# Tiles moved to whole kilobytes of SBUF, and a loop order changed in two places of a diffusion block's small matmuls

## Chip, cores and metric

The kernel runs on one core of one Trainium2 chip. The metric is the time on the device of one execution, in microseconds (us); lower is better. The profile names the engines PE (TensorE; PEld is its loading of weights), DVE (VectorE), ACT (ScalarE), POOL (GpSimd) and SP (the queue that issues most DMAs).

## What is computed

A block of two layers works on 1024 latent tokens and 256 context tokens of width 1024. The first layer is attention (differential attention in 4 heads and neighbourhood attention in 8), the second a bidirectional state-space layer (S5) followed by a GLU; both layers end in an MLP with a hidden width of 4096. Cut to the parts that matter here:

```python
# first layer: y = concat(diff_attention, neighbourhood_attention) @ w_out ; x = x + g1*y
# second layer, for both directions:
bur = einsum('blgh,gph->blgp', u, bbr); bui = einsum('blgh,gph->blgp', u, bbi)   # 64 groups of 16 channels, 64 states
s   = scan(a, bu)                                                               # complex, along the tokens
y  += einsum('blgp,ghp->blgh', sr, c_re) - einsum('blgp,ghp->blgh', si, c_im)
z   = gelu(y + d*h);  x = x + g1 * (z @ w_a) * sigmoid(z @ w_b)
# both layers:
x   = x + g2 * (square(relu(h2 @ w1)) @ w2)
```

## The kernel before

**Large products.** Every large product is made of three float32r products in `mm3` (L309 to L316): the weights and the activations are each split into a high and a low part (`w_hi`, `w_lo`; `Hh`, `Hl`, or `hid_h`, `hid_l` for the hidden layer), and hi x hi, hi x lo and lo x hi are added in PSUM. The weights are the stationary operand, 128 x 128, the activations stream past them, 512 tokens at a time (256 for the block of context tokens). Only `vv` (L541) is the other way round: there the activations are stationary and the weights stream, `wh[:, :, k]`, two runs of 128 columns, each 512 bytes in a partition. Weights come through two pools: `raw` (as loaded, 1024 columns) and `wp` (split, two buffers, L298 to L307).

**Stages.** The input projection (`in_proj`, L454; accumulators `ip_acc` and `v_acc`) runs to 512 us; between its products the generator `prep` (L1642) puts in the preparation of the state-space layer: the adaLN vectors (`ada`, L243, accumulator `ada_acc`) and, 16 times, `ssm_slice` (L1269). Then come attention (to 967 us; its order is written by a planner with costs and ranks, `Plan`, which orders each engine's work), the output projection (`op_acc`), the first MLP (`mlp`, L1120, `m_acc`), from 2036 us the scan of the state-space layer (`ssm`, L1403, planned in the same way), the GLU (`g_acc`, 2257 to 2443 us) and the second MLP. Outside the planner's stages each engine works in the order of the program.

**The lag kernels.** `ssm_slice` builds, for four groups q of 16 channels, a kernel over lags: matmuls of 64 states (rows 0 to 63 or 64 to 127 of the array, by q % 2) and 32 output channels (columns 32q of the array and partitions 32q of one PSUM tile, `sl_kp`). For each q there are three stretches of lags (128, 16 and 112 columns), each with a real and an imaginary part `ri`; operands are plain float32, which makes two instructions of each matmul. The results are copied out (`sl_ks`) and stored for the scan. The same array can hold several such small matmuls at once, each in its own tile of rows and columns.

**The scan's inputs.** In `ssm`, `xmm` (L1472) projects two groups g2 into the states of the scan: the array's columns and the PSUM partitions 64 g2, 128 rows. Direction d = 0 has one matmul of 160 tokens for each g2 and ri; d = 1 has two, of 32 and 128 tokens, read backwards.

**Where tiles lie.** SBUF is shared out by pools that grow from the left end or from the right end; a pool opened on top of others lies next to them, and tiles lie in a pool in the order of their allocation. Start addresses that the program's allocation gives, in bytes of a partition, and what they are beyond a whole kilobyte (1024 bytes):

| tiles | side | start | beyond a kilobyte |
|---|---|---|---|
| Hh, Hl of the first layer | left | 20416, 36800, ... 94144 | 960 |
| w_hi, w_lo | left | 28608, 44992, ... | 960 (each second 128 columns: 448) |
| hid_h, hid_l, both layers | left | 143296, ... 61376, ... | 960 |
| Hh, Hl of the second layer | right | 120288, 136672, 153056, 169440 | 480 |
| attention: p, k, v, q | right | 147872, ... | 416 |

Each row of 512 float32 tokens is 2048 bytes, so that all rows of a tile begin at the same offset. The constants' pool, which the change touches in `setup` (L209), lies at the left end below all others; the pool of `u_norm` (L1353, `rp`) is opened on the right before the second layer's `H1`.

Of the kernel before, what the change touches and what calls it, by code (L numbers as in the profile page):

```python
# [9 lines left out]
F32 = mybir.dt.float32  # L10
# [7 lines left out]
P = 128  # L18
# [182 lines left out]
class Net:  # L201
# [7 lines left out]
    def setup(self, es):  # L209
        nc, a = self.nc, self.a  # L210
        self.cp = es.enter_context(self.pool("const"))
        cp = self.cp
        cv = cp.tile([P, KT, 2], F32, name="cv")
        nc.sync.dma_start(cv, a["cvec"])
        self.vecs = cp.tile([P, 137], F32, name="vecs")
        nc.gpsimd.dma_start(self.vecs, a["vecs"])
        self.ident = cp.tile([P, P], F32, name="ident")
        make_identity(nc, self.ident)

        self.fold = cp.tile([P, 2], F32, name="fold")  # L220
        nc.vector.tensor_reduce(self.fold, self.ident.rearrange("p (q m) -> p m q", q=4)[:, 0:2], axis=AX.X, op=ALU.add)
        self.ones32 = cp.tile([P, 32], F32, name="ones32")
        nc.vector.memset(self.ones32, 1.0)
        self.inv32 = cp.tile([P, 1], F32, name="inv32")
        nc.vector.memset(self.inv32, 1.0 / 32.0)
        self.mhalf = cp.tile([P, 8], F32, name="mhalf")
        nc.vector.memset(self.mhalf, -0.5)
        self.act = cp.tile([P, KT, 32], F32, name="act")
        nc.vector.memset(self.act, 0.0)
        nc.scalar.activation(self.act[:, :, 0:2], cv, AF.Silu)  # L230
        self.hm = cp.tile([P, 16], F32, name="hm")
        nc.gpsimd.dma_start(self.hm, a["k_hm"])
        self.sd = cp.tile([P, 16], F32, name="sd")
        nc.gpsimd.dma_start(self.sd, a["s_d"])
        self.m = [cp.tile([P, 48, 2], F32, name=f"m{i}") for i in range(2)]
        self.G1 = [cp.tile([P, 8, 2], F32, name=f"G1_{i}") for i in range(2)]
        self.G2 = [cp.tile([P, 8, 2], F32, name=f"G2_{i}") for i in range(2)]
# [446 lines left out]
    def attention(self, at, ps):  # L684
# [20 lines left out]
                   pv=[bank[3].rearrange("p (u t) -> p u t", u=4)])  # L705
        turn = dict.fromkeys(mem, 0)
        sq = at.tile([P, P], F32, name="at_sq")

        def T(ring):
            turn[ring] += 1  # L710
# [44 lines left out]
        for h in range(4):  # L755
# [3 lines left out]
            for b, (t0, n) in enumerate(BLK):  # L759
# [4 lines left out]
                for u in range(nq):  # L764
                    st = {}
# [159 lines left out]
                o = [plan.add("S", 0.29, r + 0.5, F(g2, u=u), [o1]) for u in range(nq)]  # L925
                o = plan.add("V", 0.6, r + 1, g3, o)
                o = plan.add("G", 0.9, r + 1, g4, [o])
                o = plan.add("V", 0.47, r + 2, g5, [o])
                o = [plan.add("G", 0.35, r + 2, F(gn, u=u), [o], give=[("s0", first)]) for u in range(nq)]
                o6 = plan.add("PE", 0.11 * nq, r + 5, g6, o, take=["tp"], give=[("on", o1)])  # L930
                o = plan.add("S", 0.13 + 0.11 * nq, r + 4, g7, [o6])
# [4 lines left out]
        for pr in range(4):  # L936
# [3 lines left out]
            for rp in range(10):  # L940
                b, u = (rp // 4, rp % 4) if rp < 8 else (2, rp - 8)
# [9 lines left out]
                st = {}  # L951
# [72 lines left out]
                for hh in range(2):  # L1024
                    q = rank + (2.35 if big else 0.5) * hh
# [9 lines left out]
                for i in range((nk + 511) // 512):  # L1035
                    c, w = 512 * i, min(512, nk - 512 * i)
                    evs = []
                    for hh in range(2):
                        q = rank + 8 + 2 * i + hh
# [229 lines left out]
    def ssm_slice(self, sl, pz, ps):  # L1269

        nc, a = self.nc, self.a
        V, G = nc.vector, nc.gpsimd
        cols = slice(4 * sl, 4 * sl + 4)
        bc = pz.tile([P, 4, 4, 16], F32, name="sl_bc", tag="sl_bc", bufs=2)
        nc.sync.dma_start(bc.rearrange("p q c h -> p q (c h)"), a["s_bc"][sl])

        def big(w):
            return pz.tile([P, 576], F32, name="sl_big", tag="big", bufs=4)[:, :w]

        bb = pz.tile([P, 2, 4, 32], F32, name="sl_bb", tag="sl_bb", bufs=2)  # L1280
        V.memset(bb[:, :, :, 16:32], 0.0)
        tb = pz.tile([P, 4, 16], F32, name="sl_tb", tag="sl_tb", bufs=2)
        cf = [self.cf[:, q, cols][:, :, None].broadcast_to([P, 4, 16]) for q in range(2)]
        self.cmul(V, (bb[:, 0, :, 0:16], bb[:, 1, :, 0:16]), cf, (bc[:, 0], bc[:, 1]), tb)

        bl = [big(512).rearrange("p (a s h) -> p a s h", a=4, s=8) for _ in range(2)]
        t = big(512).rearrange("p (a s h) -> p a s h", a=4, s=8)
        sh = [P, 4, 8, 16]
        pw = [self.pB[:, q, cols][:, :, :, None].broadcast_to(sh) for q in range(2)]
        bv = [bb[:, q, :, 0:16][:, :, None, :].broadcast_to(sh) for q in range(2)]  # L1290
        self.cmul(V, bl, pw, bv, t)
        yield
        st = pz.tile([P, 4, 2, P], F32, name="sl_st", tag="sl_st", bufs=1)
        for h in range(2):
            tp = ps.tile([P, 512], F32, name="sl_tp", tag="mm")
            for q in range(4):
                nc.tensor.transpose(tp[:, P * q:P * q + P], bl[q % 2][:, 2 * h + q // 2].rearrange("p s h -> p (s h)"), self.ident)
            nc.scalar.activation(st[:, 2 * h:2 * h + 2].rearrange("p c r m -> p (c r m)"), tp, AF.Copy)
        nc.sync.dma_start(self.pD[:, 2 * sl:2 * sl + 2, 0:512], st.rearrange("p (a c) r m -> p a (c r m)", a=2))

        nci = pz.tile([P, 4, 16], F32, name="sl_nci", tag="sl_nci", bufs=2)
        V.tensor_scalar(nci, bc[:, 3], -1.0, None, op0=ALU.mult)
        sh = [P, 4, 9, 16]
        w = pz.tile([P, 4, 2, 144], F32, name="sl_w", tag="sl_w", bufs=1)
        wv = w.rearrange("p c r (j h) -> p r c j h", j=9)
        t = [big(576).rearrange("p (a j h) -> p a j h", a=4, j=9) for _ in range(2)]
        pw = [self.pC[:, q, cols][:, :, :, None].broadcast_to(sh) for q in range(2)]
        cr, ci, ni = (x[:, :, None, :].broadcast_to(sh) for x in (bc[:, 2], bc[:, 3], nci))
        G.tensor_tensor(wv[:, 0], pw[0], cr, ALU.mult)
        V.tensor_tensor(t[0], pw[1], ci, ALU.mult)  # L1310
        G.tensor_tensor(wv[:, 0], wv[:, 0], t[0], ALU.subtract)
        G.tensor_tensor(wv[:, 1], pw[0], ni, ALU.mult)
        V.tensor_tensor(t[1], pw[1], cr, ALU.mult)
        G.tensor_tensor(wv[:, 1], wv[:, 1], t[1], ALU.subtract)
        nc.sync.dma_start(self.pD[:, 2 * sl:2 * sl + 2, 512:1088], w.rearrange("p (a c) r m -> p a (c r m)", a=2))
        yield

        kp = ps.tile([P, 512], F32, name="sl_kp", tag="mm")
        for q in range(4):
            o, ln = kp[32 * q:32 * q + 32], slice(64 * (q % 2), 64 * (q % 2) + 64)  # L1320
            c = 2 * (q // 2)
            for lo, hi, d, w0, start, stop in ((0, 128, 1, 16, True, False), (112, 128, 0, 0, False, True), (128, 240, 0, 16, True, True)):
                for ri in range(2):
                    nc.tensor.matmul(o[:, lo:hi], bb[ln, ri, c + d], w[ln, c + d, ri, w0:w0 + hi - lo], start=start and ri == 0,
                                     stop=stop and ri == 1, skip_group_check=True)
        ks = pz.tile([P, 240], F32, name="sl_ks", tag="sl_ks", bufs=2)
        V.tensor_copy(ks, kp[:, :240])
        V.scalar_tensor_tensor(ks[:, 112:128], self.hm, self.sd[:, sl:sl + 1], ks[:, 112:128], op0=ALU.mult, op1=ALU.add)
        for q in range(4):
            nc.sync.dma_start(self.KD[:, 4 * sl + q], ks[32 * q:32 * q + 16])  # L1330
        yield
# [21 lines left out]
    def u_norm(self, rp, sp, ps):  # L1353
# [5 lines left out]
        for q, v in enumerate((self.G1[1], self.m[1][:, 0:8])):  # L1359
            nc.sync.dma_start(gD[q].rearrange("c g h m -> (g h) c m"), v)  # L1360
        self.gU = rp.tile([P, 2, 64, 2], F32, name="gU")
        for s in range(8):
            for q in range(2):
                nc.sync.dma_start(self.gU[16 * s:16 * s + 16, q], gD[q].rearrange("c g h m -> h (c g) m"))
# [38 lines left out]
    def ssm(self, sp, ps):  # L1403
# [24 lines left out]
        for pair in range(32):  # L1428
# [43 lines left out]
            def xmm(st=st, pair=pair, ct=ct, pl=pl):  # L1472
                bl = st["par"][:, 0:512].rearrange("p (d r m) -> p d r m", d=2, r=2)
                st["U"] = U_of[ct]
                X = st["X"] = T("X")
                for ri in range(2):
                    for d in range(2):
                        for g2 in range(2):
                            U = st["U"][:, 2 * pl + g2]

                            for c, u in ((0, U),) if d == 0 else ((160, U[:, 31::-1]), (192, U[:, 159:31:-1])):
                                PE.matmul(X[64 * g2:64 * g2 + 64, ri, c:c + u.shape[1]], bl[:, d, ri, 64 * g2:64 * g2 + 64], u,
                                          start=True, stop=True, skip_group_check=True)

# [242 lines left out]
```

## Time and profile before

| | us |
|---|---|
| median of 3 runs | 3184.99 (3183.87 to 3185.97) |
| profiled execution | 3183.76 |
| its span, first to last instruction | 3181.7 |
| PE busy in the span | 2997.4 (94%), 17736 matmuls |
| DVE, POOL, ACT busy | 1848.8, 1129.1, 969.6 |
| mean granted clock of TensorE | 0.978 of full speed |

A row of a group gives line, engine, operation, what is written and read, shape and count; then the busy time, the mean length of one in ns, and the engine's idle time before them. Matmuls are pipelined: the length of one goes on while the next has begun, so that the time that one costs is read from start to start. A row of the timeline gives the start, the length, the instruction and how many of the line stand together there. A row of a stretch gives its length, then for each engine the busy time and the count, the granted clock, the DMA engines' share and GB/s.

### The profile page before, as it was taken

How to read it: one execution, taken by the hardware profiler on the slowest of the kernel's cores; microseconds unless marked ns; L12 is line 12 of the kernel's file. 1: busy time of each engine (PE TensorE's matmuls, PEld its weight loads, DVE VectorE, ACT ScalarE, POOL GpSimd, SP SyncE). 2: the span in 40 equal slices, each digit the busy share in tenths (PEclk: the TensorE clock that was granted, in tenths of full speed). 3: DMA queues.
4: the chain of work that ended last, by engine and by line, in shares of the span. 5: the costliest groups of instructions: out<-in, count | busy, mean ns of one | idle time of the engine just before them, and what ended most of it. 6: DMA issues, size and time to landing. Idle time of an engine off the chain costs nothing.

```text
span 3181.7 us, 46326 instructions
## 1 busy us (share of the span) xinstructions
PE 2997.4 (94%) x17736; PEld 2470.1 (78%) x17736; DVE 1848.8 (58%) x3225; ACT 969.6 (30%) x1843; POOL 1129.1 (35%) x2314
## 2 busy tenths in 40 slices
PE   7999998888999999999999999777899999999998
PEld 4878888777878777877888888566677888888886
DVE  4886575998663555445555454599524544455444
ACT  3321114766663311221111211455323212111122
POOL 3352123555442377778785000377323000000001
PEclk8999999999999999999999999888999999999999
DMA  6355565233543133333311111666212111111111
GB/s 234 106 195 200 198 203 151 67 89 101 153 113 133 60 124 104 117 104 110 60 62 53 34 33 38 165 186 177 85 60 86 48 45 53 40 54 48 45 53 53
DMA packets 171150, 321.55 MB, mean 101 GB/s; under 512 B 34560, under 2 KB 97056, under 8 KB 170928
## 3 DMA queue, kind: packets, MB, share of 16 engines
q1 hardware_dynamic: 165840, 302.24, 30.9%
q0 software_dynamic: 5088, 16.34, 1.7%
q8 instruction: 140, 2.29, 0.3%
q14 instruction: 82, 0.67, 0.1%
HBM read 253.03 MB, written 65.49 MB: 100 GB/s over the span
## 4 chain that ended last, share of the span: by engine, by line
PE 67%; DVE 10%; issue 2%; ACT 2%; DMA 2%; POOL 1%; SPq 0%; DVEq 0%; POOLq 0%; ACTq 0%
PE m_acc L314 17%; PE m_acc L315 16%; PE m_acc L316 16%; PE at_bank L736 2%; DVE s_ab L1501 2%; PE at_sc L728 2%; PE g_acc L314 2%; PE g_acc L316 2%; PE g_acc L315 2%; PE at_bank L1019 2%; DVE s_ab L1489 1%; PE at_bank L846 1%; PE ada_acc L266 1%; PE op_acc L316 1%; DVE s_s L1514 1%
## 5 line engine op out<-in xcount | busy, mean ns | idle before, releaser
L1087 DVE SCALAR_TENSOR_TENSOR xl<-m_acc,m,xl 128x512 f32<-128x512 f32 x512 | 379.1, 748 | 222.3 <-PE m_acc L316 221.6
L314 PE MATMUL m_acc<-Hh,w_hi 128*128 128x512 f32 (+1 forms) x1280 | 476.1, 372 | 0.9 <-ACT Hh L450 0.9
L314 PE MATMUL m_acc<-hid_h,w_hi 128*128 128x512 f32 (+1 forms) x1280 | 476.8, 372 | 0.0
L315 PE MATMUL m_acc<-Hl,w_hi 128*128 128x512 f32 (+1 forms) x1280 | 474.4, 371 | 0.5 <-DVE Hl L451 0.5
L316 PE MATMUL m_acc<-Hh,w_lo 128*128 128x512 f32 (+1 forms) x1280 | 474.1, 370 | 0.0
L315 PE MATMUL m_acc<-hid_l,w_hi 128*128 128x512 f32 (+1 forms) x1280 | 471.9, 369 | 0.0
L316 PE MATMUL m_acc<-hid_h,w_lo 128*128 128x512 f32 (+1 forms) x1280 | 471.6, 368 | 0.0
L305 ACT ACTIVATE w_hi<-w_raw 128x1024 fp32r<-128x1024 f32 x196 | 202.6, 1053 | 803.7 <-PE m_acc L315 691.5
L306 DVE TENSOR_TENSOR w_lo<-w_raw,w_hi 128x1024 fp32r<-128x1024 f32 x196 | 243.6, 1257 | 219.9 <-ACT w_hi L305 210.3
L1138 DVE TENSOR_TENSOR m_r<-m_r 128x512 f32<-128x512 f32 (+1 forms) x160 | 105.7, 662 | 414.2 <-ACT hid_h L1137 413.9
L422 POOL TENSOR_TENSOR rs_y<-n_v,mhalf 128x4 f32<-128x4 f32 (+1 forms) x13 | 12.4, 950 | 772.5 <-DVE n_v L370 772.5
L314 PEld LDWEIGHTS m_acc<-hid_h,w_hi 128*128 128x128 f32 x1280 | 241.0, 188 | 56.8 <-issue 15.3
L314 PEld LDWEIGHTS m_acc<-Hh,w_hi 128*128 128x128 f32 x1280 | 241.2, 188 | 50.2 <-issue 5.8
L315 PEld LDWEIGHTS m_acc<-hid_l,w_hi 128*128 128x128 f32 x1280 | 241.3, 188 | 44.7 <-issue 5.0
L315 PEld LDWEIGHTS m_acc<-Hl,w_hi 128*128 128x128 f32 x1280 | 241.3, 188 | 44.4 <-DVE Hl L451 2.1
L316 PEld LDWEIGHTS m_acc<-Hh,w_lo 128*128 128x128 f32 x1280 | 241.2, 188 | 43.6
L316 PEld LDWEIGHTS m_acc<-hid_h,w_lo 128*128 128x128 f32 x1280 | 241.2, 188 | 40.8
L1136 ACT ACTIVATE m_r<-m_acc 128x512 f32<-128x512 f32 (+1 forms) x160 | 88.0, 552 | 447.7 <-PE m_acc L316 443.8
L314 PE MATMUL ip_acc<-Hh,w_hi 128*128 128x512 f32 (+1 forms) x384 | 141.7, 370 | 4.0 <-ACT Hh L450 4.0
L315 PE MATMUL ip_acc<-Hl,w_hi 128*128 128x512 f32 (+1 forms) x384 | 138.5, 361 | 1.2 <-DVE Hl L451 1.2
L316 PE MATMUL ip_acc<-Hh,w_lo 128*128 128x512 f32 (+1 forms) x384 | 137.7, 359 | 0.0
L728 PE MATMUL at_sc<-at_k,at_q 128*128 128x256 f32 (+2 forms) x608 | 125.4, 337 | 10.9 <-ACT at_p L818 5.1
(346 smaller groups left out, 5908.9 us busy)
## 6 DMA issues: line engine op xcount, KB each, us to landing
w_raw<-in_w_dram SPq DMA_DIRECT2D x128, 512.0 KB, 4.0
ada_raw<-in_wada_dram SPq DMA_DIRECT2D x96, 512.0 KB, 4.2
s_par<-pD SPq DMA_DIRECT2D x32, 864.0 KB, 4.6
at_q<-qD SPq DMA_DIRECT2D x152, 128.0 KB, 2.8
w_raw<-in_win_dram SPq DMA_DIRECT2D x24, 512.0 KB, 4.6
pD<-tb_cs POOLq DMA_DIRECT2D x32, 320.0 KB, 2.6
pD<-sl_w SPq DMA_DIRECT2D x16, 576.0 KB, 3.2
at_k<-kD SPq DMA_DIRECT2D x28, 320.0 KB, 5.8
```

The lines of the kernel that those rows point to most:

```text
L305: nc.scalar.activation(hi[:, j], r, AF.Copy)
L306: nc.vector.tensor_tensor(lo[:, j], r, hi[:, j].bitcast(F32), ALU.subtract)
L314: nc.tensor.matmul(out, lh, rh, start=first and i == 0, stop=False)
L315: nc.tensor.matmul(out, lh, rl, start=False, stop=False)
L316: nc.tensor.matmul(out, ll, rh, start=False, stop=last and i == n - 1)
L728: PE.matmul(sc[:, c:c + n], qd["q"][:, m, hl, qo:qo + P], k["k"][m][:, k0:k0 + n], start=(hl == 0), stop=(hl == 1))
L736: PE.transpose(tp[:kw, P * j:P * j + P], p[:, c0 + P * j:c0 + P * j + kw], self.ident)
L1019: PE.matmul(grp["pv"][64 * hh:64 * hh + 64, u, :], hd["v"][:kw, vt, 64 * hh:64 * hh + 64], st["aT", (hh, i)][:kw, P * (j % 4):P * (j % 4) ...
L1087: nc.vector.scalar_tensor_tensor(xv, av, gate, xv, op0=ALU.mult, op1=ALU.add)
L1136: nc.scalar.activation(r[:, :n], acc[:, :n], AF.Relu)
L1138: nc.vector.tensor_tensor(r[:, :n], r[:, :n], r[:, :n], ALU.mult)
L1501: V.tensor_tensor_scan(R, dec, R, 0.0, op0=ALU.mult, op1=ALU.add)
```

## The change

Four tiles are allocated that nothing writes or reads: 64 bytes of a partition at the start of the constants (left), 992 bytes in a pool of their own at the right end, 448 bytes at the end of the attention's pool and 512 bytes in the pool `rp`. The left tiles thereby move up by 64 bytes, from 960 to 0 beyond a kilobyte (the weights' second halves from 448 to 512). The right tiles move down by 992 bytes, those of the attention by 992 + 448 = 1440, from 416 to 0, and the second layer's Hh and Hl by 992 + 512 = 1504, from 480 to 0. In the lag kernels the loop over the four groups q becomes the innermost; in the scan's inputs the loop over the two groups g2 does. The same matmuls are issued with the same operands, in another order.

```diff
         cp = self.cp
+
+        cp.tile([P, 16], F32, name="pad_l")
+        es.enter_context(self.pool("pad", side="right")).tile([P, 248], F32, name="pad_r")
...
         sq = at.tile([P, P], F32, name="at_sq")
+        at.tile([P, 112], F32, name="at_pad")
...
-        for q in range(4):
-            o, ln = kp[32 * q:32 * q + 32], slice(64 * (q % 2), 64 * (q % 2) + 64)
-            c = 2 * (q // 2)
-            for lo, hi, d, w0, start, stop in ((0, 128, 1, 16, True, False), (112, 128, 0, 0, False, True), (128, 240, 0, 16, True, True)):
-                for ri in range(2):
+        for lo, hi, d, w0, start, stop in ((0, 128, 1, 16, True, False), (112, 128, 0, 0, False, True), (128, 240, 0, 16, True, True)):
+            for ri in range(2):
+                for q in range(4):
+                    o, ln = kp[32 * q:32 * q + 32], slice(64 * (q % 2), 64 * (q % 2) + 64)
+                    c = 2 * (q // 2)
                     nc.tensor.matmul(o[:, lo:hi], bb[ln, ri, c + d], w[ln, c + d, ri, w0:w0 + hi - lo], start=start and ri == 0,
                                      stop=stop and ri == 1, skip_group_check=True)
...
         self.gU = rp.tile([P, 2, 64, 2], F32, name="gU")
+        rp.tile([P, 128], F32, name="pad_u")
...
                     for d in range(2):
-                        for g2 in range(2):
-                            U = st["U"][:, 2 * pl + g2]
-
-                            for c, u in ((0, U),) if d == 0 else ((160, U[:, 31::-1]), (192, U[:, 159:31:-1])):
+
+                        for c, ks in ((0, slice(0, 160)),) if d == 0 else ((160, slice(31, None, -1)), (192, slice(159, 31, -1))):
+                            for g2 in range(2):
+                                u = st["U"][:, 2 * pl + g2, ks]
                                 PE.matmul(X[64 * g2:64 * g2 + 64, ri, c:c + u.shape[1]], bl[:, d, ri, 64 * g2:64 * g2 + 64], u,
                                           start=True, stop=True, skip_group_check=True)
```

## Rows read from the trace of the kernel before

**Rows 1.** the head of the page

```profile
span 3181.7 us, 46326 instructions
```

**Rows 2.** busy time of the engines in four stretches; PEclk is the granted share

```profile
200.00:520.00 320.00, 310.46 (x2555) 266.55 (x2552) 208.54 (x334) 64.60 (x122) 89.91 (x68) 0.99 0.58 194
2036.00:2258.00 222.00, 157.02 (x1218) 131.96 (x1218) 207.34 (x316) 108.41 (x239) 149.48 (x160) 0.84 0.59 158
2258.00:2443.00 185.00, 183.71 (x792) 146.86 (x792) 58.04 (x65) 52.51 (x70) 48.04 (x32) 0.99 0.27 86
2443.00:3165.00 722.00, 717.69 (x3136) 579.03 (x3135) 358.90 (x475) 154.19 (x218) 19.44 (x19) 1.00 0.14 46
```

**Rows 3.** PE in order of time, second layer (start us, length us)

```profile
2800.05 0.39 PE L314 MATMUL m_acc<-hid_h,w_hi 128*128 128x512 f32 x1
...
2804.59 0.39 PE L316 MATMUL m_acc<-hid_h,w_lo 128*128 128x512 f32 x1
2804.81 0.40 PE L314 MATMUL m_acc<-Hh,w_hi 128*128 128x512 f32 x1
...
2814.85 0.40 PE L315 MATMUL m_acc<-Hl,w_hi 128*128 128x512 f32 x1
```

**Rows 4.** PE in order of time, first layer

```profile
1299.64 0.39 PE L314 MATMUL m_acc<-Hh,w_hi 128*128 128x512 f32 x1
...
1301.91 0.39 PE L315 MATMUL m_acc<-Hl,w_hi 128*128 128x512 f32 x1
```

**Rows 5.** groups of L314, whole execution; L315 and L316 have as many

```profile
L314 PE MATMUL m_acc<-hid_h,w_hi 128*128 128x512 f32 (+1 forms) x1280 | 476.8, 372 | 0.0
L314 PE MATMUL m_acc<-Hh,w_hi 128*128 128x512 f32 (+1 forms) x1280 | 476.1, 372 | 0.9 <-ACT Hh L450 0.9
...
L314 PE MATMUL ip_acc<-Hh,w_hi 128*128 128x512 f32 (+1 forms) x384 | 141.7, 370 | 4.0 <-ACT Hh L450 4.0
...
L314 PE MATMUL g_acc<-Hh,w_hi 128*128 128x512 f32 x256 | 102.2, 399 | 1.8 <-ACT w_hi L305 1.8
...
L314 PE MATMUL v_acc<-w_hi,Hh 128*128 128x256 f32 x320 | 93.6, 293 | 0.0
...
L314 PE MATMUL op_acc<-Hh,w_hi 128*128 128x512 f32 (+1 forms) x192 | 68.6, 357 | 1.9 <-DVE xc L1087 1.9
```

**Rows 6.** one group by shape, second layer; L315 and L316 have as many

```profile
L314 PE MATMUL m_acc<-Hh,w_hi 128*128 128x512 f32 x512 | 202.6, 396 | 0.9 <-ACT Hh L450 0.9
```

**Rows 7.** PE in order of time, a v_acc product

```profile
256.93 0.28 PE L314 MATMUL v_acc<-w_hi,Hh 128*128 128x256 f32 x1
...
258.60 0.28 PE L316 MATMUL v_acc<-w_hi,Hl 128*128 128x256 f32 x1
```

**Rows 8.** PE in order of time, around one burst of L1324

```profile
284.81 0.39 PE L316 MATMUL ip_acc<-Hh,w_lo 128*128 128x512 f32 x1
285.12 2.90 PE L1324 MATMUL sl_kp<-sl_w,sl_bb 64*32 64x128 f32 x48
287.95 0.43 PE L282 MATMUL ada_tp<-ident,ada_e 32*128 32x32 f32 x4
288.31 0.39 PE L314 MATMUL ip_acc<-Hh,w_hi 128*128 128x256 f32 x1
```

**Rows 9.** the same burst by shape

```profile
L1324 PE MATMUL sl_kp<-sl_w,sl_bb 64*32 64x128 f32 x16 | 2.4, 275 | 0.0
L1324 PE MATMUL sl_kp<-sl_w,sl_bb 64*32 64x112 f32 x16 | 2.2, 257 | 0.0
L1324 PE MATMUL sl_kp<-sl_w,sl_bb 64*32 64x16 f32 x16 | 1.1, 178 | 0.0
```

**Rows 10.** PE in order of time, sl_tp and ada_acc

```profile
254.93 1.03 PE L1297 MATMUL sl_tp<-ident,sl_big 128*128 128x128 f32 x8
255.90 0.64 PE L266 MATMUL ada_acc<-ada_raw,act 128*32 128x256 f32 x8
256.47 0.39 PE L314 MATMUL v_acc<-w_hi,Hh 128*128 128x256 f32 x1
```

## The prediction

> **What bounds the kernel.** The profiled execution took 3183.8 us, 2.1 us of it around a span of 3181.7 us [rows 1]; the median of the runs is 3185.0 us, 1.2 us more, and is the base of the sums. A change under 0.2% (6.4 us) cannot be told from none. I read first the engines' busy time in the four stretches in which the change edits or realigns most of the work [rows 2]. In the input projection's main part (200 to 520 us) TensorE is busy 310.5 of 320 us, 97%, VectorE 65%. In the GLU and the second layer's MLP (2258 to 3165 us) TensorE is busy 901.4 of 907 us, 99%, VectorE 46%. There a saved TensorE nanosecond is a saved nanosecond. In the scan (2036 to 2258 us) it is the other way: VectorE 207.3 of 222 us, TensorE 157.0 us.
>
> Next I read the spacing of large products, start to start, because the durations of a matmul (0.39 us) overlap. In the second layer, products that stream the hidden tiles start every (2804.59 - 2800.05) / 20 = 0.2270 us, and those that stream Hh and Hl right behind them every (2814.85 - 2804.81) / 43 = 0.2335 us [rows 3]: same shape, same granted clock (1.00, the 2.4 GHz level), same weights pool. In the first layer Hh and Hl stream at (1301.91 - 1299.64) / 10 = 0.227 us [rows 4]. What differs is the address: the slow tiles begin 480 bytes beyond a whole kilobyte, the fast ones 960. 480 is no multiple of 64, 960 is.
>
> **The pads, right side.** They move the second layer's Hh and Hl from 480 to 0. Products concerned: 3 x 512 in the MLP [rows 6] and 3 x 256 in the GLU [rows 5], 2304. I price 0 like 960: 2304 x 0.0065 = 15.0 us, all on TensorE's path. The ends: nothing, and a start every 0.213 us (512 columns at 2.4 GHz, one a clock, by the granted clock of [rows 2]), 2304 x 0.0205 = 47 us. I take the nearest row, the same instruction at another offset.
>
> **The pads, left side.** Everything else that streams (first layer's Hh, Hl and weights, hidden tiles of both layers) goes from 960 to 0. All large products are 3 x 3712 = 11136 [rows 5], so 8832 here. No row shows an operand on a whole kilobyte. The nearest: in v_acc the moving operand is two runs of 512 bytes, which start in turn at 960 and at 448 beyond a kilobyte for even and odd k, so that the runs cross a kilobyte in one case and not in the other. Both have one spacing: (258.60 - 256.93) / 14 = 0.119 us [rows 7], no unevenness by thirds. Crossing a kilobyte costs nothing there. I take 0; the ends are 0 and 11 ns each (0.119 against 256 columns in 0.107 us, about the same for 512), 97 us.
>
> The Trainium skill (SBUF — State Buffer, Specifications) tells of cachelines of 16 bytes in SBUF. By it 960, 480 and 0 would all be alike, and every pad would give 0; the 0.227 against 0.2335 us above does not fit it. It is rival 2.
>
> **The lag kernels' matmuls (L1324).** A burst stands between two other products: the last ip_acc starts at 284.81, the burst at 285.12 (0.31 us, 0.085 more than a spacing, the price of a change of tiling), and it lasts 2.83 us [rows 8]. Its 48 instructions are 16 each of 128, 112 and 16 columns [rows 9], since every f32 product is two. Eight f32 products of 128 columns take 0.97 - 0.085 us, 0.111 us each [rows 10]; 112 columns then 0.097; 16 columns 0.035 (an estimate: half of the 32-column ada_tp, (0.36 - 0.085) / 4 = 0.069 [rows 8]). One after the other that is 16 x (0.111 + 0.097 + 0.035) = 3.89 us. The burst has 2.745 without the leaving, so neighbours in different tiles of the array already overlap, at the three places where q changes. With q innermost neighbours always differ. What four column groups do abreast shows in ada_acc, whose loop has its four q inside: 8 instructions of 256 columns, 8 x 0.222 = 1.78 us in a row, start to the next product in 0.57 - 0.085 = 0.485 us, 3.65 abreast [rows 10]. So a burst becomes 3.89 / 3.65 + 0.085 = 1.15 us, or 1.06 with four abreast; two abreast would be 2.03. I take 1.10: 1.73 x 16 bursts = 27.7 us, times the 97% of TensorE's share = 27 us. Behind the burst on TensorE's queue are the projections' products, which have operands ready; next in line is VectorE with 65%, which would rise to 71%. The copies out of this PSUM tile wait for its last product and come earlier.
>
> The Trainium skill (TensorEngine Tiling (Array Packing), Gotcha 1: PSUM Pressure) says that different row tiles cannot access the same PSUM bank at the same time. The four groups alternate between rows 0 to 63 and 64 to 127 and write one bank. By that rule no neighbours would overlap, a burst would last 3.97 us, and the kernel would end at 3185 + 1.14 x 16 x 0.97 - 15 = 3188 us. The burst of 2.745 against 3.89 us contradicts it, since only such neighbours meet in it.
>
> **The scan's inputs and the rest.** The reordering in xmm saves TensorE time where VectorE has 93% of the stretch [rows 2] and the planner's order stays: 0, at most the 14.7 us that VectorE leaves, and nearest to 0 for that reason. The attention's pad touches 256 score products of 512 columns by the code: 0, at most 256 x 0.0065 = 1.7 us. No instruction, transfer or wait is added; the pads have none. Shifted tiles keep their neighbours on either side but for the pads, so I cost the reuse of memory at 0.
>
> **Sum.** 3183.8 - 15 - 27 = 3141.8 us for the profiled execution, 3143 us for the median.
>
> **Rivals.**
> 1. Whole kilobytes are faster than 960 too. For: all fast rows lie 64 bytes short of one, none on one; 0.227 is still above 0.213. Against: v_acc [rows 7]. Price: 6.5 ns on all 11136 more, 72 us, gives 3071; the full 11 ns 122 us, gives 3021.
> 2. The offset is not what slows the second layer, or the pads don't cure it: 3185 - 27 = 3158. Against: [rows 3, 4].
> 3. Only two groups run abreast, as where q changes now: a burst of 2.03, 0.8 x 16 x 0.97 = 12.4 us, gives 3157.
> 4. Slower: every change of row group costs TensorE the 0.085 us of a change of tiling, in the burst itself. 24 pairs have 23 changes, 3.89 + 24 x 0.085 = 5.93 us a burst, 3.1 x 16 x 0.97 = 48 us more, gives 3218. It decides once a burst passes 2.83 + 15 / 15.5 = 3.8 us. Against: the three changes inside the present burst, which is shorter than its sum.
>
> **Numbers.** Forecast 0.70; rival 1 0.12; rival 2 0.08; rival 3 0.05; rival 4 0.03; the row tiles that exclude each other 0.02, which is the case of no change. Faster 0.95, same 0.02, slower 0.03. The forecast's own range is 3135 (four abreast, 5 us from the scan, 1.7 from the scores) to 3154 (new waits take a third of the bursts' gain). Rivals 2 and 3 lie at 3158 and 3157, with which 0.83 is held; to 3165 if waits take part of theirs, and down to 3122, a tenth of rival 1's price and some.
>
> **What would show it.** In the changed profile: second layer Hh products every 0.227 us, the mean of 396 ns [rows 6] some 6 ns lower; first layer unchanged at 0.227; sl_kp x48 about 1.1 us long; input projection some 27 us shorter, the scan within 5 us. It is wrong if the first layer's spacing falls, if the burst stays above 2 us, or if TensorE's idle time before 520 us grows by more than 10 us.

## The result, and the profile after

The changed kernel takes 3135.8 us (median of 4 runs, 3131.91 to 3141.85) against 3184.43 us before in the same session (4 runs, 3182.77 to 3185.97): ratio 0.9849, 95% interval 0.9831 to 0.9867, 48.6 us less. The forecast was 3143 us.

The profiled execution took 3133.75 us. Its head, and the busy time in four stretches laid where the stages now are (columns as in [rows 2]):

```profile
span 3132.0 us, 46329 instructions
```

```profile
200.00:484.00 284.00, 277.36 (x2522) 236.00 (x2521) 200.22 (x323) 60.19 (x113) 88.13 (x66) 0.99 0.62 209
2004.00:2222.00 218.00, 153.81 (x1216) 129.91 (x1215) 205.03 (x312) 106.49 (x236) 149.39 (x160) 0.85 0.55 158
2222.00:2403.00 181.00, 179.61 (x793) 147.23 (x794) 58.59 (x65) 53.07 (x70) 47.96 (x32) 0.99 0.28 88
2403.00:3114.00 711.00, 707.00 (x3136) 579.61 (x3134) 358.37 (x474) 153.89 (x218) 18.93 (x18) 1.00 0.14 47
```

The limits are where they were: TensorE 98% in the input projection (VectorE 70%, forecast 71%) and 99% behind the scan, VectorE 94% in the scan. What became shorter is seen by cutting both traces at the starts of TensorE's first or last instruction of each stage (us, each cut rounded to 0.1):

| stretch | before | after | less |
|---|---|---|---|
| start to the first burst of L1324 | 197.3 | 196.3 | 1.0 |
| to the first matmul of attention (16 bursts) | 315.0 | 287.5 | 27.5 |
| attention | 454.7 | 451.6 | 3.1 |
| output projection | 119.5 | 119.0 | 0.5 |
| first MLP, to its last product | 938.8 | 939.2 | -0.4 |
| to the first product of the GLU (scan) | 232.1 | 228.3 | 3.8 |
| GLU | 185.4 | 180.9 | 4.5 |
| second MLP, to its last product | 721.4 | 711.0 | 10.4 |
| the end | 17.5 | 18.2 | -0.7 |
| span | 3181.7 | 3132.0 | 49.7 |

The two forecast terms are there, 27.5 us (forecast 27) and 4.5 + 10.4 = 14.9 us (forecast 15.0). Another 7 us are not in the forecast, and most of them lie in two rows, attention and the scan.

TensorE in order of time, second layer, a batch of 48 hidden products and one of 48 of Hh and Hl (answers to [rows 3]), and two products of the first layer (answer to [rows 4]):

```profile
2748.99 0.39 PE L317 MATMUL m_acc<-hid_h,w_hi 128*128 128x512 f32 x1
...
2759.64 0.39 PE L319 MATMUL m_acc<-hid_h,w_lo 128*128 128x512 f32 x1
2759.87 0.39 PE L317 MATMUL m_acc<-Hh,w_hi 128*128 128x512 f32 x1
...
2770.53 0.39 PE L319 MATMUL m_acc<-Hh,w_lo 128*128 128x512 f32 x1
```

```profile
1267.11 0.39 PE L317 MATMUL m_acc<-Hh,w_hi 128*128 128x512 f32 x1
...
1269.83 0.39 PE L317 MATMUL m_acc<-Hh,w_hi 128*128 128x512 f32 x1
```

Hidden (2759.64 - 2748.99) / 47 = 0.2266 us, Hh and Hl (2770.53 - 2759.87) / 47 = 0.2268 us, first layer (1269.83 - 1267.11) / 12 = 0.2267 us. The second layer's 0.2335 us is gone, and on a whole kilobyte nothing is faster than at 960. The group by shape in the second MLP (answers to [rows 6]) has its mean 6 ns lower:

```profile
L317 PE MATMUL m_acc<-Hh,w_hi 128*128 128x512 f32 x512 | 199.7, 390 | 0.9 <-ACT Hh L453 0.9
```

And a burst of the lag kernels, TensorE in order of time (answers to [rows 8]):

```profile
277.07 0.39 PE L319 MATMUL ip_acc<-Hh,w_lo 128*128 128x512 f32 x1
277.39 1.15 PE L1328 MATMUL sl_kp<-sl_w,sl_bb 64*32 64x128 f32 x48
278.48 0.43 PE L285 MATMUL ada_tp<-ident,ada_e 32*128 32x32 f32 x4
```

It lasts 278.48 - 277.39 = 1.09 us in place of 2.83.

### The profile page after: what moved, and what is told of

Its sections match the earlier page's. It is cut to its first block, busy times and chain, and to the rows that moved or that the text cites. A ratio compares the mean times of both kernels' runs of the same rounds, so it can differ in the third digit from the quotient of the medians.

```text
span 3132.0 us, 46329 instructions
## 1 busy us (share of the span) xinstructions
PE 2949.1 (94%) x17736; PEld 2435.7 (78%) x17736; DVE 1844.6 (59%) x3225; ACT 969.1 (31%) x1843; POOL 1128.4 (36%) x2314
## 4 chain that ended last, share of the span: by engine, by line
PE 77%; DVE 13%; issue 3%; DMA 3%; ACT 2%; POOL 2%; SPq 0%; DVEq 0%; POOLq 0%; ACTq 0%
PE m_acc L317 17%; PE m_acc L318 16%; PE m_acc L319 16%; DVE s_ab L1506 2%; PE at_bank L740 2%; PE at_sc L732 2%; PE g_acc L319 2%; PE g_acc L317 2%; PE g_acc L318 2%; PE ip_acc L317 2%; PE ada_acc L269 2%; PE ip_acc L318 2%; PE ip_acc L319 2%; PE at_bank L1023 2%; DVE s_ab L1494 1%
```

## The experiments

Each run's time is compared with the kernel before on the same chip. Spacings are means over whole batches of 48 products of 512 columns in the second MLP (15 or 30 batches in a run, alike within 0.8 ns for one distance of the operands).

**1. The lag kernels' order alone.** The kernel before with one hunk of the change:

```diff
-        for q in range(4):
...
+        for lo, hi, d, w0, start, stop in ((0, 128, 1, 16, True, False), (112, 128, 0, 0, False, True), (128, 240, 0, 16, True, True)):
+            for ri in range(2):
+                for q in range(4):
...
```

> The kernel before with the loop order of the lag kernels alone. Theory: the 16 bursts of 48 instructions fall from 2.83 us to the 1.08 us that the changed kernel shows, 16 x 1.75 = 28 us, and the time falls by 27 to 28 us, to about 3157 us; the second layer's Hh products stay at 0.2335 us. Rival, the pads share in it (tiles moved on the left shorten the bursts): bursts above 1.3 us here and less than 22 us gained. Rival, the unexplained 7 us of the changed kernel come from this edit too (PE ahead earlier, so that later stages start better): 35 us gained.

Measured: 3159.62 us (3153.73 to 3161.19), ratio 0.9917 (0.9903 to 0.9931), 25.2 us less. The 16 bursts last 1.08 us each, as in the changed kernel, so the order does it alone; second layer Hh stay at 233.35 ns. The stretch of the bursts is 289.7 us long, 25.3 less than before.

**2. The scan's order alone.**

```diff
-                        for g2 in range(2):
...
+                        for c, ks in ((0, slice(0, 160)),) if d == 0 else ((160, slice(31, None, -1)), (192, slice(159, 31, -1))):
+                            for g2 in range(2):
...
```

> The kernel before with the loop order of the scan's inputs alone. Theory: bursts of 24 stay between 1.36 and 1.42 us and the time within 2 us of 3184 us, since VectorE bounds the scan. Rival: the unexplained 4 us between the first MLP and the scan come from it: then 3180 us, and the first burst of the scan stands 4 us nearer to the end of the first MLP.

Measured: 3184.48 us, ratio 0.9999 (0.9991 to 1.0008). TensorE in order of time, a burst of `s_X` before, and one in this run:

```profile
2092.15 1.49 PE L1482 MATMUL s_X<-s_U,s_par 128*64 128x160 f32 x24
```

```profile
2087.72 1.43 PE L1482 MATMUL s_X<-s_U,s_par 128*64 128x160 f32 x24
```

The reordered burst is 0.06 us shorter by its row, 32 x 0.06 = 2 us of TensorE in the whole scan, and nothing of it shows in the time. Its gain was put at 0, and is. The first `s_X` stays 14.0 us behind the MLP, so that the rival is out.

**3. The pads alone.** The changed kernel with both loop orders of the kernel before.

```diff
-        for lo, hi, d, w0, start, stop in ((0, 128, 1, 16, True, False), (112, 128, 0, 0, False, True), (128, 240, 0, 16, True, True)):
-            for ri in range(2):
-                for q in range(4):
...
+        for q in range(4):
...
-                        for c, ks in ((0, slice(0, 160)),) if d == 0 else ((160, slice(31, None, -1)), (192, slice(159, 31, -1))):
-                            for g2 in range(2):
...
+                        for g2 in range(2):
...
```

> The changed kernel without its two loop orders, so the four pads alone. Theory: 2304 products from 0.2335 to 0.227 us, 15 us, to about 3169 us. If the unexplained 7 us of the changed kernel belong to the pads (3 us in the attention, whose tiles move from 416 to 0, and 4 us ahead of the scan), 3162 us; if they are the spread between runs or belong to the loop orders, 3169 us. Rival, pads do nothing alone: 3184 us.

Measured: 3164.91 us (3158.99 to 3166.86), ratio 0.9935 (0.9922 to 0.9947), 19.9 us less. With run 1 that is 25.2 + 19.9 = 45.1 of the 48.6 us: the parts add up within the spread of the runs. The first `s_X` of the scan starts 9.5 us behind the start of the first MLP's last product, 14.0 before: the extra microseconds ahead of the scan belong to the pads.

**4. Only the second layer's Hh and Hl, by 32 bytes.**

```diff
         self.gU = rp.tile([P, 2, 64, 2], F32, name="gU")
+        rp.tile([P, 8], F32, name="pad_u")
```

> The kernel before with one tile of 32 bytes of a partition added in the pool ahead of the second layer's Hh and Hl, which moves those from 480 to 448 beyond a kilobyte and nothing else that streams in large products. Theory (a start on a multiple of 64 bytes is what counts, not a whole kilobyte): their 2304 products start every 0.227 us and the time falls by 15 us, to 3169 us. Rival (a whole kilobyte, or 64 bytes short of one, is needed; or 256 bytes): they stay at 0.2335 us and the time at 3184 us.

Measured: 3170.8 us (3165.41 to 3175.67), ratio 0.9954 (0.994 to 0.9967), 14.1 us less; Hh and Hl start every 226.67 ns, GLU 180.5 us, second MLP 711.2 us. The whole 15 us come from 32 bytes and need no whole kilobyte. The first `s_X` stays 14.0 us behind the MLP.

**5. Lag kernels and 32 bytes at the right end, in place of four pads.** The kernel of run 1 and:

```diff
         cp = self.cp
+        es.enter_context(self.pool("pad", side="right")).tile([P, 8], F32, name="pad_r")
```

> The kernel before with the loop order of the lag kernels and one tile of 32 bytes of a partition at the right end, in place of the change's four pads (2016 bytes): every right tile moves down by 32 bytes, the second layer's Hh and Hl from 480 to 448 beyond a kilobyte, the latents from 992 to 960, the attention's tiles from 416 to 384; left tiles stay at 960, the scan's inputs in the old order. Theory (what the pads give is a start on a multiple of 64 bytes for tiles on the right side, no whole kilobyte, and the left pad and the scan's order give nothing): as fast as the whole change, 3132 to 3142 us. Rival (whole kilobytes, or the left pad, give part of it): 3145 us or more.

Measured: 3143.86 us (3138.66 to 3147.97), ratio 0.987 (0.9853 to 0.9888). Nearly the change: the median is 8 us longer, but the intervals of the two ratios overlap (0.9853 to 0.9867), so that the times alone leave it open whether anything is missing. The stages say more. GLU and MLP are as in the changed kernel (181.0 and 711.0 us); the stretch of the scan is 231.9 us against 228.3, with the first `s_X` 14.0 us behind the MLP. So something ahead of the scan is not cured by a multiple of 64 on the right; run 11 takes it up.

**6. The left tiles at 32 beyond a kilobyte.** The run that upset the explanation:

```diff
-        cp.tile([P, 16], F32, name="pad_l")
+        cp.tile([P, 24], F32, name="pad_l")
```

> The changed kernel with a left pad of 96 bytes in place of 64, so that every left tile that streams (first layer's Hh and Hl, the weights, the hidden tiles) begins 32 beyond a kilobyte in place of 0; the right side stays. Theory (off a multiple of 64 bytes a 512-column product costs 0.2335 in place of 0.227 us): 0.0065 us on those of the 8832 products on the left that have 512 columns, and perhaps as much on those with 256, 40 to 57 us, to about 3180 us. Rival (only a whole address range or the right side matters, or 16 bytes are enough): 3136 us as the changed kernel.

Measured: 3154.04 us (3152.12 to 3156.84), ratio 0.9902 (0.9887 to 0.9917), 18 us more than the changed kernel. Neither expectation holds. TensorE in order of time, the hidden products at 32, then a batch of Hh and Hl, which still stand on a whole kilobyte:

```profile
2764.71 0.39 PE L317 MATMUL m_acc<-hid_h,w_hi 128*128 128x512 f32 x1
...
2775.36 0.39 PE L319 MATMUL m_acc<-hid_h,w_lo 128*128 128x512 f32 x1
...
2786.79 0.40 PE L317 MATMUL m_acc<-Hh,w_hi 128*128 128x512 f32 x1
...
2797.76 0.40 PE L319 MATMUL m_acc<-Hh,w_lo 128*128 128x512 f32 x1
```

The tiles that were moved off a multiple of 64 keep (2775.36 - 2764.71) / 47 = 0.2266 us; those left on a whole kilobyte go up to (2797.76 - 2786.79) / 47 = 0.2334 us. The first layer's products, whose activations moved as well, keep the 0.227 us of the changed kernel. What moved with these tiles is the weights, from 0 to 32. So the operand's own address is not what counts; its distance to the weights may be.

**7. Four offsets at once**, weights at 0. Second layer's Hh and Hl at 16 and 4 bytes, hidden tiles at 32 and 8:

```diff
...
+                w = [hp.tile([P, KT * 512 + 256], F32R, name=f"H{x}{b}") for b in blocks]
+                setattr(net, "H" + x, [t[:, o:o + KT * 512].rearrange("p (k n) -> p k n", k=KT) for t, o in zip(w, (4, 1))])
...
+                    o = (8, 2)[b]
+                    hh, hl = (mp.tile([P, 2 * n + 256], F32R, name=f"hid_{x}", tag=f"h{x}{b}", bufs=1)[:, o:o + 2 * n].rearrange("p (j n) -> p j n", j=2)
+                              for x in "hl")
```

> The changed kernel with four offsets in the second layer: Hh and Hl of its first block of 512 tokens at 16 bytes beyond a multiple of 64, of its second block at 4 bytes; the hidden tiles of its MLP at 32 bytes for the first block and at 8 for the second. Theory (64 bytes): all four sets of products start every 0.2335 us, the second MLP gets (1536 + 1536) x 0.0065 = 20 us longer and the GLU 5 us. Rival (lines of 16 bytes): 16 and 32 give 0.227, 4 and 8 give 0.2335 us. Rival (cost grows with the offset or by its alignment): the four spacings differ.

Measured: 3166.72 us (one run). 32 bytes: 233.4 ns, 8 bytes: 233.2, 16 bytes: 231.7, 4 bytes: 237.4, the last in these rows:

```profile
2793.23 0.39 PE L317 MATMUL m_acc<-Hh,w_hi 128*128 128x512 f32 x1
...
2804.39 0.40 PE L319 MATMUL m_acc<-Hh,w_lo 128*128 128x512 f32 x1
```

None is free, and they differ by the offset (32 and 8 by 0.2 ns only), the third expectation.

**8. The order 0, 2, 1, 3 of the groups.**

```diff
-                for q in range(4):
+                for q in (0, 2, 1, 3):
```

> The changed kernel with the four groups of a lag kernel taken in the order 0, 2, 1, 3, so that neighbours in the queue share their rows of the array twice in four, where in the change each neighbour has other rows. All write one PSUM bank. Theory (tiles of other rows and columns run abreast whatever the order): bursts of 48 stay at 1.08 us. Rival (row tiles hinder each other in one bank): bursts shorter than 1.0 us, or, if tiles that share rows hinder each other, longer than 1.3 us.

Measured: 3136.09 us (one run). TensorE in order of time:

```profile
278.35 1.15 PE L1328 MATMUL sl_kp<-sl_w,sl_bb 64*32 64x128 f32 x48
279.43 0.43 PE L285 MATMUL ada_tp<-ident,ada_e 32*128 32x32 f32 x4
```

1.08 us again. Taken one by one, the starts in this trace and in that of the change come in fours: four instructions 5 to 8 ns apart, and, where they have 112 or 128 columns, another 75 to 115 ns before the next four begin. So four groups run abreast, each in 32 partitions of its own of one PSUM bank, whichever of them share their rows.

**9. Weights at 32, Hh and Hl at 992**: both 32 off a multiple of 64, 192 apart modulo 256. Run 6 and:

```diff
-        rp.tile([P, 128], F32, name="pad_u")
+        rp.tile([P, 136], F32, name="pad_u")
```

> The run with the left tiles at 32 beyond a kilobyte, and now the second layer's Hh and Hl at 992 in place of 0 as well, so that weights and activations all stand 32 bytes off a multiple of 64. New theory (what counts is the moving operand's place modulo 64 bytes against that of the weights, not its own address): all 512-column products start every 0.227 us, and the time is that of the changed kernel, 3132 to 3142 us. Rival, the theory of the prediction (a start off a multiple of 64 is slow by itself): the second layer's products stay at 0.2335 us or more, the time 3150 us or more.

Measured: 3154.03 us (3152.02 to 3155.31), ratio 0.99 (0.9884 to 0.9917), and in the second layer

```profile
2788.04 0.39 PE L317 MATMUL m_acc<-Hh,w_hi 128*128 128x512 f32 x1
...
2799.00 0.40 PE L319 MATMUL m_acc<-Hh,w_lo 128*128 128x512 f32 x1
```

(2799.00 - 2788.04) / 47 = 0.2332 us. The new theory, distance modulo 64, falls too.

**10. Distances of 64 to 256 bytes**, weights at 0, tiles shifted as in run 7: second layer's Hh and Hl 64 and 128 on, hidden tiles 192 and 256, the context block of the first layer 32.

```diff
...
+            w = [(hp.tile([P, KT * BLK[b][1] + 64], F32R, name=f"H{x}{b}"), BLK[b][1], ((16, 32) if len(blocks) == 2 else (0, 0, 8))[j]) for j, b in enumerate(blocks)]
+            setattr(net, "H" + x, [t[:, o:o + KT * n].rearrange("p (k n) -> p k n", k=KT) for t, n, o in w])
...
+                    o = (48, 64)[b]
```

> The changed kernel with other distances between activations and weights (weights at 0 modulo 64): second layer's Hh and Hl of the first block 64 bytes on, of the second 128; hidden tiles of the second MLP 192 and 256 bytes on; and the first layer's Hh and Hl of the context block (256 columns) 32 bytes on. New theory (distance modulo 64): the first four all at 0.227 us, the MLP as long as in the changed kernel, 711 us; the context block's products, if a shorter stream pays the same, 0.1265 in place of 0.120 us. Rival (a distance of 128, 256 or 512 is needed): 0.2335 us at 64, 128, 192.

Measured: 3148.45 us (one run). 64 bytes: 229.2 ns (uneven, mostly 225 to 232 by product), 128: 232.5 (228 to 241), 192: 233.3, 256: 227.1. TensorE in order of time, hidden products at 256:

```profile
2757.68 0.39 PE L317 MATMUL m_acc<-hid_h,w_hi 128*128 128x512 f32 x1
...
2768.35 0.39 PE L319 MATMUL m_acc<-hid_h,w_lo 128*128 128x512 f32 x1
```

A distance of 256 is free and no smaller one is: the rival was right, with 256. The context's products of 256 columns, 32 apart, did not become slower but start every 0.117 to 0.118 us (medians by stage) in place of 0.120.

**11. The latents at 512, the context at 128 beyond a kilobyte**, all else as in the changed kernel. `xl` and `xc` are what the copies L1397 and L1399 write to memory (`xS`) ahead of the scan; before they lay 992 beyond a kilobyte, in run 5 at 960, in the changed kernel at 0.

```diff
+        xp.tile([P, 128], F32, name="pad_x0")
         self.xl = xp.tile([P, KT, 8, 128], F32, name="xl")
+        xp.tile([P, 160], F32, name="pad_x1")
         self.xc = xp.tile([P, KT, 8, 32], F32, name="xc")
+        xp.tile([P, 224], F32, name="pad_x2")
```

> The changed kernel with the latents xl at 512 bytes beyond a kilobyte and the context xc at 128, both in place of 0; all tiles that large products read stay. Theory (the copies of x to memory ahead of the scan read runs of 512 bytes, of xc 128 bytes, and what counts is that a run stays within one unit of its own size): landing medians as in the changed kernel, 5.6 and 4.9 us for xl, 8.4, 6.4 and 5.8 for xc, and 9 to 10 us from the last product of the first MLP to the first of the scan. Rival (a whole kilobyte is needed): 6.7 and 6.1 us, 8.9, 8.7 and 8.3, and 14 us, as in the kernel before.

Measured: 3139.6 us (one run). The DMA issues of three of the five groups of these copies (KB each, median us from issue to landing): before, then run 5 (960), the changed kernel (0), and this run:

```profile
xS<-xl POOLq DMA_DIRECT2D x3, 1024.0 KB, 6.7
xS<-xc POOLq DMA_DIRECT2D x1, 384.0 KB, 8.7
xS<-xc POOLq DMA_DIRECT2D x1, 128.0 KB, 8.3
```

```profile
xS<-xl POOLq DMA_DIRECT2D x3, 1024.0 KB, 6.7
xS<-xc POOLq DMA_DIRECT2D x1, 384.0 KB, 8.6
xS<-xc POOLq DMA_DIRECT2D x1, 128.0 KB, 8.3
```

```profile
xS<-xl POOLq DMA_DIRECT2D x3, 1024.0 KB, 5.6
xS<-xc POOLq DMA_DIRECT2D x1, 384.0 KB, 6.4
xS<-xc POOLq DMA_DIRECT2D x1, 128.0 KB, 5.8
```

```profile
xS<-xl POOLq DMA_DIRECT2D x3, 1024.0 KB, 5.6
xS<-xc POOLq DMA_DIRECT2D x1, 384.0 KB, 6.1
xS<-xc POOLq DMA_DIRECT2D x1, 128.0 KB, 5.8
```

The 128 KB copy, the first of `xc`, lands 2.5 us earlier on 0 and on 512 with 128, and not on 960. The gain of the others is smaller, down to 0.4 us for the last copy of `xc` (512 KB: 8.9 before, 8.5 after). The 128 KB copy is on the path: the scan's first load reads what it and the copies of `xl` wrote, and the chain of work that ended last, as the profile follows it back, goes through it, before and after:

```profile
2019.68 8.30 DMA xS<-xc
```

```profile
1987.96 5.81 DMA xS<-xc
```

The waits between the first MLP and the scan, before and after (`s_par` is loaded behind `s_U` on one queue):

```profile
PE s_X L1482 <- DMA s_par<-pD: 8.5, 1, 8.5
DVE s_U L1438 <- DMA s_U<-xS: 7.6, 1, 7.6
```

```profile
PE s_X L1487 <- DMA s_U<-xS: 4.3, 1, 4.3
DVE s_U L1443 <- DMA s_U<-xS: 3.4, 1, 3.4
```

The first `s_X` follows the MLP by 9.5 us here; over all profiles by 9.3 to 10.1 us in the nine kernels with `xl` on 0 or 512, and by 13.9 to 14.1 in the five with it at 992 or 960. The copy explains 2.5 of these 4 us. The rest comes behind it, where the eight DMAs of the first load are issued within 3.65 us in place of 6.28; why is not shown, and the tiles that they write lie on the left, which moved in the same nine kernels. The whole stretch to the GLU is only 2.6 us shorter in the nine (mean 228.8 us against 231.4): the chain that ended last then waits longer for the scan's second load of `s_U` (8.57 us after, 6.23 before).

**12. Everything 32 off a multiple of 256.** Run 6, and:

```diff
-        rp.tile([P, 128], F32, name="pad_u")
+        rp.tile([P, 312], F32, name="pad_u")
...
+                t = hp.tile([P, KT * 256 + 64], F32R, name=f"H{x}2")
+                w.append(t[:, 8:8 + KT * 256].rearrange("p (k n) -> p k n", k=KT))
...
```

> The changed kernel with weights, activations and hidden tiles of both layers all 32 bytes beyond a multiple of 256: the left side at 32 beyond a kilobyte (weights too), the second layer's Hh and Hl at 288. The first layer's Hh and Hl of the context block stand 32 bytes further, 64 beyond a multiple of 256. Theory (what counts is the distance between moving operand and weights modulo 256 bytes, and 0 gives 0.227 us): all products of 512 columns start every 0.227 us though none stands on a multiple of 64, the GLU lasts 181 and the second MLP 711 us; the context's products fall from 0.120 to 0.117 us as in the run with the second sweep, 1344 x 0.003 = 4 us at most, so 3130 to 3140 us. Rival (own address on a multiple of 256, or of 64): second layer at 0.233 us or more, 3150 us or more.

Measured: 3136.54 us (3135.1 to 3140.68), ratio 0.9856 (0.9839 to 0.9874), the time of the changed kernel.

```profile
2774.59 0.39 PE L317 MATMUL m_acc<-Hh,w_hi 128*128 128x512 f32 x1
...
2785.24 0.39 PE L319 MATMUL m_acc<-Hh,w_lo 128*128 128x512 f32 x1
```

(2785.24 - 2774.59) / 47 = 0.2266 us with no operand of these products on a multiple of 64; GLU 180.7, second MLP 711.0 us. The context's 0.118 us gave nothing that shows: the first MLP lasts 939.3 us here and 937.7 in run 10, 939.2 in the changed kernel. No run is faster than the changed kernel beyond the spread.

## Why the prediction was right, and where it was not

All spacings, by the distance of activations to weights (start of the one less start of the other, modulo 256 bytes):

| distance | where | ns, start to start |
|---|---|---|
| 0 | the change; runs 4, 5, 12; hidden tiles of run 6 | 226.7 to 226.9 |
| 256, which is 0 modulo 256 | run 10 | 227.1 |
| 4 / 8 / 16 | run 7 | 237.4 / 233.2 / 231.7 |
| 32 | before, second layer; run 7 | 233.4 |
| 64 / 128 | run 10 | 229.2 / 232.5 |
| 192 | runs 9 and 10 | 233.3 |
| 224 | run 6, second layer | 233.3 |

- **Right pads, 15.0 us: right in size, wrong in reason.** The step "What differs is the address ... 480 is no multiple of 64, 960 is" failed. In [rows 3] the fast and the slow tiles differ in a second thing, which the table of places ahead of the prediction holds: the weights start at 960 or 448. The hidden tiles are 0 or 512 away from them, Hh and Hl 480 - 960 = -480, which is 32 modulo 256. Runs 6, 9 and 12 part the two readings: an activation on a whole kilobyte is slow (233.3) with weights at 32, one at 288 is fast (226.7) with them. That the size came out is luck in the layout: the change takes weights and activations to 0 together, so that either reading gave 15.0 us; 14.9 were measured.
- **Left pads, 0: right**, and again since activations and weights move together. Runs 4 and 5 leave the left side at 960 and have 226.7 ns as well.
- **Rival 1** (a whole kilobyte beats 960) is out by [rows 4] against the row of after, 0.227 both, **rival 2** by run 4. By the Trainium skill (SBUF — State Buffer, Specifications) SBUF is read in cachelines of 16 bytes; distances of 16, 32, 64 and 128 bytes, all whole lines, cost 2.5 to 6.7 ns here, so that the measurement decides against lines of 16 as what counts here.
- **Lag kernels, 1.10 us a burst and 27 us: right.** 1.08 us in every burst, 16 x 1.75 = 28.0 us, and the stretch is 27.5 us shorter (25.1 to 27.5 in the kernels with this order). Four abreast, read off `ada_acc` [rows 10], carried over to tiles with other rows. Its reading of the burst before holds too: by the single starts, the four instructions of 112 columns that end a group run beside the first four of the next, 3 x 4 x 0.097 = 1.16 us, and 3.89 - 2.745 = 1.15 us were missing. **Rivals 3 and 4** (2.03 and 5.93 us) are out. The Trainium skill (TensorEngine Tiling (Array Packing), Gotcha 1: PSUM Pressure) has different row tiles not access one PSUM bank at the same time; 1.08 us with all four groups in one bank, in either order (run 8), speaks against it here, where each group writes partitions of its own.
- **The scan's inputs, 0: right** (run 2), with VectorE at 94% of the stretch.
- **"No instruction, transfer or wait is added"** is the step that missed 3 us. True of the count; but the pads move tiles that transfers read, and the price of a transfer was taken to be the same at any address. The copies of `xl` and `xc` land up to 2.5 us earlier (run 11), and the scan's stretch is 3.8 us shorter. The sign "the scan within 5 us" was met, but not by the reordering, which gave nothing (run 2). So 3135.8 us lies inside the range, just above its lower end of 3135, partly by luck: of the 5 us that this end allowed for the reordering in the scan none came, and the copies, which the sum did not have, gave some 3. The Trainium skill (DMA: Bandwidth & Descriptors, How a descriptor splits into AXI transactions) says that a transaction must start at a multiple of 256 bytes, so that a piece which begins elsewhere fetches bytes that it doesn't use. By that rule a run of 512 bytes at 992 takes 23 beats of 32 bytes in place of 16, an estimate from the page; the traces agree in direction (6.7 against 5.6 us, 1.2 times, slow at 960 and 992, fast at 0 and 512), and none of them singles out 256.
- **The other 3 us, in attention, are spread.** Over the fourteen profiles attention lasts 451.6 to 455.7 us, and the kernels with the change's placement of its tiles stand at both ends (after 451.6, run 7 455.7); what sets it in one execution is not shown. The forecast's 3141.8 for the profiled execution, less 2.6 to 3.8 for the copies and 3.1 for attention, is 3135 to 3136; 3133.75 was measured.

What stays open is why the distance matters. Weights are loaded while activations stream: in the second MLP the loads are busy for 579.6 of 711 us beside TensorE's 707.0 (the last row of the stretches after). That the two reads get in each other's way fits all the runs, but no run streamed without loading, and whether it is the product's own weights or the next one's that count was not tried. Nor was `xl` moved back alone: run 4 parts it from the second layer's Hh and Hl, but the left tiles stood at 960 in all five kernels with slow copies. The copies neither read nor write a left tile, so that their own price is read from their rows.

## What to carry to other kernels

When two groups of the same matmul differ by some nanoseconds, write down the start of every operand, the stationary one too, before naming the cause; placing activations and weights a multiple of 256 bytes apart cost 32 bytes of a partition here (run 4) and gave 14 us. When tiles are moved, look at the transfers that read or write them as well as at the engines. In bursts of small matmuls that use different tiles of the array, try the loop over the tiles innermost: 2.83 us became 1.08 here.

## What had not been expected

- A 512-column product costs 226.7 to 237.4 ns by where its two operands lie to each other, longest at 4 bytes of the distances tried; 256-column products get 2 to 3 ns shorter at a distance of 32, where 512-column ones get 6.7 longer.
- Even at distance 0 a product costs 13 ns more than one column a clock at 2.4 GHz would take (226.7 against 213 for 512 columns, 120 against 107 for 256).
- The same copy from SBUF to memory (`xc`, 128 KB) takes 8.3 us in the five kernels with the tile that it reads at 992 or 960, and 5.8 in the nine with it on 0 or 128.
